# Mixer: weight casts issued apart from their low parts, with the decays, the gate's sigmoid and the first state in another order; X's scale in the FFNs on VectorE

## The chip, the cores and the metric

The kernel runs on one core of one Trainium2 chip. The metric is the time of one execution in device microseconds, the median of several runs.

## The reference

Two layers, each with the same weights for 128 context tokens and 256 latent tokens (384 in all, width 1024): an FFN, a mixer, an FFN. Every one of the three is modulated by shift, scale and gate rows made from a conditioning vector, and is closed by a LayerNorm over `alpha*x + gate*w*f(mod(x))`.

```python
def _layer(x, cond, p, lb, ctx):
    mod = (silu(cond) @ p["w_mod"] + p["b_mod"])
    sh1, sc1, g1, sh2, sc2, g2, sh3, sc3, g3 = split(mod, 9)
    f1 = _swiglu(_modulate(x, sh1, sc1), p["ffn1_w_in"], p["ffn1_w_out"])
    x = _layer_norm(ALPHA * x + 0.5 * g1 * f1, ...)
    y, new = _mixer(_modulate(x, sh2, sc2), p, lb, ctx)
    x = _layer_norm(ALPHA * x + g2 * y, ...)
    f2 = _swiglu(_modulate(x, sh3, sc3), p["ffn2_w_in"], p["ffn2_w_out"])
    return _layer_norm(ALPHA * x + 0.5 * g3 * f2, ...), new

def _mixer(h, p, lb, ctx):
    zq, zi, zff, zfb, zg, zglu, cq, ck, cv = split(h @ p["w_in"])
    # gated linear recurrence, forward and backward: S_t = f_t S_{t-1} + (1 - f_t) v_t^T, o_t = S_t^T q_t
    # f = lb + (1 - lb) * sigmoid(zff or zfb)
    # convolution module: depthwise_conv(glu_a * sigmoid(glu_b)), LayerNorm, silu
    # grouped-query attention with RMS norms and rotary positions
    y = concat([o_a, o_conv, o_c]) @ p["w_out"]
```

Outputs are the tokens, the new keys and values of the context, and the final states of the recurrence.

## The kernel before

All products run on TensorE in a two-part form: a float32 operand is split into a high part, a cast to the reduced type `F32R` by ScalarE (`split_to`, L584), and a low part, the rest, by VectorE (L585). A product is three matmuls per tile of 128: high by high, low by high, high by low. `aform` (L594) gives 24 matmuls of 384 columns for one weight part of 128 outputs (8 tiles deep); `entry_mm` (L638) gives 24 matmuls of 256 columns for one token tile.

The order of the instructions on TensorE, VectorE, ScalarE and GpSimd is the order of the program text. Only the DMA queue SP is ordered by the framework. Each engine works its queue strictly in that order; an instruction that waits holds what is behind it.

**FFN.** `ffn` runs over 22 units of 128 hidden columns. In unit `u` the program issues `prep(u + 1)` (casts and low parts of the next unit's gate, up and output weights), `fill(u)`, from unit 4 the scale of X (`finish_x`: six operations on the three token tiles, in every FFN but the first), then the gate and up products of the unit, `act` (silu on ScalarE L740, product `hf` on VectorE L742, cast L744 and low part L745) and the output product `out` of the unit before (L607). The products of a unit land in two PSUM banks that take turns (`wbank`).

`fill` makes the modulation rows of later sub-layers beside this. First it moves on every piece that is finished with its sum (`finish_job`: products with the selector `sel` on TensorE L212, a sum `rows` on VectorE L220, and in the unit after it transposes and two copies). Then it does as many steps of the next piece as the plan says; a step is two operations of 128x1024 on VectorE (L198 or L200). `SLOW` is two steps a unit over four units, `FAST` three, two, three.

**Mixer.** `load(g)` brings 256 columns of the input weight into one of four `raw` buffers, `prep(n)` splits half of them into weight part `W[n]` in one of four `wgu` buffers and, after an odd `n`, loads the next. `gemm(n)` multiplies part `n`. The parts in turn: 0 to 3 the two forget gates, 4 and 5 the queries `q`, 6 and 7 the gate half of the convolution's input (their sigmoid goes to `ua`), 8 to 11 values, keys and values of the attention for each token tile (`entry_mm` into `pkv`), 12 and 13 the other half of the convolution's input, 14 and 15 the output gate.

`Dec` holds the decays of one pair of heads. `sums(d)` is a running sum, a copy and a difference on VectorE and three exponentials on ScalarE; `keys` and `queries` are three and two VectorE operations per direction; `level(h)` copies keys and queries of blocks of `h` on ScalarE and scales them on VectorE. `dec[0]` goes through levels 8, 16, 32 and 64 before the loop over token tiles, `dec[1]` through 8 and 16 before it and 32 and 64 in it.

The loop `for i in range(2 * NT + 1)` (L1456 on) runs `scores(i)` (small products, then four masked copies on VectorE), `outputs(i - 1)`, two convolutions (`conv`, at i = 2 and 4) and other work. In it the first state is made: `state_turn(0)` transposes keys on TensorE and copies them to `kN` on ScalarE at i = 0, `states(0, kN)` multiplies them with the values `vN` at i = 1. `conv_load` writes the convolution's input `u` to memory and reads it back in another layout.

Of the kernel before, what the change touches and what calls it, by code (L numbers as in the profile page):

```python
# [9 lines left out]
F32 = mybir.dt.float32  # L10
F32R = mybir.dt.float32r
U8 = mybir.dt.uint8
AF = mybir.ActivationFunctionType
ALU = mybir.AluOpType
# [30 lines left out]
class Net:  # L45
# [195 lines left out]
    def fill(self, u, pool):  # L241

        for g in list(self.fin):
            if next(g, self) is self:
                self.fin.remove(g)
        for _ in range(self.plan.get(u, 0)):
            self.step(*self.todo.pop(0), pool)
# [248 lines left out]
    def finish_tok(self, gb, tok):  # L496
        x = self.X[:, tok, :]
        self.nc.gpsimd.tensor_tensor(x, x, gb[:, 0, :], ALU.mult)
        self.nc.gpsimd.tensor_tensor(x, x, gb[:, 1, :], ALU.add)
# [160 lines left out]
    def ffn(self, l, st, eps, nxt, fillers):  # L660
# [5 lines left out]
        with self.tc.tile_pool(name=self.name("ffn"), bufs=1, reuse_waits="tile") as fp:  # L666
# [103 lines left out]
            for u in range(2, NU):  # L770
                if u + 1 < NU:
                    prep(u + 1)
                self.fill(u, fp)
                if u == 4 and (l, st) != (0, 0):
                    self.finish_x(l - (st == 0), 2 if st == 0 else 1)
                wg, wu, _ = wsp[u]
                pg, pu = self.wbank(), self.wbank()
                self.aform(pg[:, 0:T], wg)
                if u == 2:
                    if not first:  # L780
                        turn01(1)
                        turn01(2)
                        acc = [self.pair(i) for i in self.ord]
                self.aform(pu[:, 0:T], wu)
                if u == NU - 1 and nxt is not None:
                    res = nxt(0)
                act(u, pg[:, 0:T], pu[:, 0:T])
                if first and u in (3, 6):
                    if u == 3:
                        rest = self.setup2(fp)  # L790
                    next(rest, None)
                if u == 2 and not first:
                    out(0, range(NT))
                if u - 1 < NU - hold and not (first and u == 2):
                    out(u - 1, range(NT))
            self.fill(NU, fp)
# [16 lines left out]
    def mixer(self, l, eps, nxt):  # L813
# [19 lines left out]
        def load(g):  # L833
            raws[g] = self.t(self.rawp, [P, KT, 256], "raw")
            nc.sync.dma_start(raws[g].rearrange("p k n -> p (k n)"), wi[l, cols[g]])

        def prep(n, lo, pool=None):
            g, i = divmod(n, 2)
            src = raws[g][:, 4 * i : 4 * i + 4, :] if g in (4, 5, 7) else raws[g][:, :, i * P : i * P + P]
            W[n] = self.split(pool or self.wgu, src, "wgu", lo)  # L840
            if i == 1 and g + 4 < len(cols):
                load(g + 4)

# [139 lines left out]
        for n in range(4):  # L983
            lc = slice(2 * l + n % 2, 2 * l + n % 2 + 1)
            nc.scalar.activation(
                sgf[:, n, :], sgf[:, n, :], AF.Ln, scale=self.lb1[:, lc], bias=self.lb[:, lc]
            )
        nc.vector.tensor_scalar_max(sgf, sgf, LN_MIN)
# [281 lines left out]
        prep(7, nc.vector)  # L1270
        dec[0].keys(0, E[0])
        E.append(dec[1].sums(0))
        gemm(5, ps=pq[:, 1, :])
        nc.scalar.copy(q[:, 1, :], pq[:, 1, :])
        prep(8, nc.vector)
        dec[0].keys(1, E[1])
        E.append(dec[1].sums(1))
        prep(9, nc.vector)
# [3 lines left out]
        gemm(7, ps=pu[:, 1, :])  # L1282
        for d in range(2):
            dec[0].queries(d)
        dec[0].level(8)
        nc.scalar.activation(ua[:, :, 0:T], pu, AF.Sigmoid)
        exp_table()
        prep(10, nc.vector)
        prep(11, nc.vector)
# [11 lines left out]
        two = lambda c, lo, hi: pkv[c][:, 0, :].rearrange("p (t n) -> p t n", t=2)[:, :, lo:hi]  # L1301
        nc.scalar.copy(vN[:, 0:2, :], two(0, 0, 256))
        nc.scalar.copy(vN[:, 2, :], pkv[0][:, 1, 0:256])
        prep(12, nc.vector)
        prep(13, nc.vector)
# [3 lines left out]
        nc.scalar.copy(kv[:, 2, :], pkv[1][:, 1, P:256])  # L1309
        for tok in range(NT):  # L1310
            k_ss.append(head_ssq(kn[:, tok, :], 2, self.t(mp, [P, P], "t1k", bufs=2)))
        cw = self.t(self.rawp, [P, 2048], "raw")
        nc.sync.dma_start(cw, a["conv_blk"][l])
        cw = cw.rearrange("p (a j m c) -> p a j m c", a=2, j=4, m=8)
        for ct in range(2):
            ps = gemm(12 + ct)
            nc.vector.tensor_mul(u[:, ct, 15:143], ps[:, 0:P], ua[:, ct, 0:P])
            nc.vector.tensor_mul(u[:, ct, 158:414], ps[:, P:T], ua[:, ct, P:T])
            conv_load(ct)
        dec[1].keys(0, E[2])  # L1320
        dec[1].keys(1, E[3])
        for d in range(2):
            dec[1].queries(d)
        dec[1].level(8)
        dec[1].level(16)
# [26 lines left out]
        S1s = []  # L1352

# [102 lines left out]
        for i in range(2 * NT + 1):  # L1456
            if i < 2 * NT:
                scores(i)
            if i in (1, NT + 1):
                S1s.append(states(i // NT, kN))  # L1460
            if i in (0, NT):
                kN = state_turn(i // NT)
# [143 lines left out]
    def run(self):  # L1606
        def plan(u0, *patterns):
# [5 lines left out]
            (0, 2): ([(0, 8)] + [(1, p) for p in range(4)], plan(3, FAST, FAST, SLOW, SLOW, SLOW)),  # L1613
# [110 lines left out]
```

## Time and profile before

| what | value |
|---|---|
| median of 3 runs | 1592.35 us (1592.04 to 1595.43) |
| profiled execution | 1594.68 us, span 1592.9 us |
| TensorE matmul busy | 1528.8 us, 96% of the span |
| VectorE busy | 1083.6 us, 68% |
| ScalarE busy | 615.3 us, 39% |
| GpSimd busy | 127.6 us, 8% |
| mean granted clock of TensorE | 0.982 |

The table shows each engine's busy time in the one profiled execution. Matmul ends are modelled, so a busy TensorE is not TensorE at its peak. The first layer's mixer lies between about 320 and 545 us of the span, the second's between about 1100 and 1325; the four FFNs lie around them. A granted clock of 1 is 2.4 GHz, one of 0.5 is 1.2 GHz.

### The profile page before, as it was taken

The numbers are of one execution on the slowest core, as the hardware profiler recorded it, in microseconds if no ns is written. First come the engines' busy times: TensorE is split into PE (matmuls) and PEld (weight loads), VectorE is DVE, ScalarE is ACT, GpSimd is POOL, SyncE is SP. The second block draws the span as 40 slices with busy tenths as digits, with TensorE's granted clock in tenths as the row PEclk, the third lists the DMA queues.
The fourth block names the chain that finished last, engine by engine and source line by source line (L and its number), as shares of the span: only waits on it lengthen the run. The fifth ranks groups of instructions, "written<-read, shape, count | busy, mean of one in ns | idle before, by whom it ended". The sixth has DMA issues, their size and how long they took to land.

```text
span 1592.9 us, 24588 instructions
## 1 busy us (share of the span) xinstructions
PE 1528.8 (96%) x10079; PEld 1375.4 (86%) x10079; DVE 1083.6 (68%) x1518; ACT 615.3 (39%) x1071; POOL 127.6 (8%) x123
## 2 busy tenths in 40 slices
PE   6999999998899999999999999999988999999997
PEld 5989999897677998899989999998985779999996
DVE  4788878677666798777776777765756675654335
ACT  2333222366365622333253323224643745232231
POOL 0000000120002040000013000001200023000001
PEclk9999999998899999999999999999989999999999
DMA  9776756412434456664534566542326034543411
GB/s 360 268 262 222 262 191 246 159 62 106 92 108 159 158 177 234 225 221 176 212 132 184 206 219 200 205 167 93 117 72 177 28 132 173 224 150 141 158 54 40
DMA packets 63080, 269.71 MB, mean 169 GB/s; under 512 B 9128, under 2 KB 13688, under 8 KB 47864
## 3 DMA queue, kind: packets, MB, share of 16 engines
q1 hardware_dynamic: 62968, 268.15, 47.9%
q8 instruction: 79, 1.29, 0.3%
q14 instruction: 33, 0.27, 0.1%
HBM read 265.09 MB, written 3.03 MB: 168 GB/s over the span
## 4 chain that ended last, share of the span: by engine, by line
PE 73%; DVE 14%; ACT 4%; DMA 4%; issue 4%; SPq 0%; POOL 0%; DVEq 0%; POOLq 0%; ACTq 0%
PE w L594 37%; PE d L607 19%; PE d L638 7%; DVE G L200 3%; DVE wgu L585 2%; DMA raw<-ffn_w_out 2%; PE w L946 2%; ACT wgu L584 2%; DMA raw<-w_mod_first 1%; DMA raw<-ln_b 1%; PE w L638 1%; PE w L413 1%; DVE wo L585 1%; PE w L212 1%; PE d L1170 1%
## 5 line engine op out<-in xcount | busy, mean ns | idle before, releaser
L594 PE MATMUL w<-xh,wgu 128*128 128x384 f32 x2752 | 719.6, 336 | 5.8 <-DVE hf L742 3.5
L594 PEld LDWEIGHTS w<-xh,wgu 128*128 128x128 f32 x2752 | 498.6, 188 | 16.4 <-DVE hf L742 6.4
L594 PE MATMUL w<-xl,wgu 128*128 128x384 f32 x1376 | 460.3, 335 | 0.0
L585 DVE TENSOR_TENSOR wgu<-raw,wgu 128x1024 fp32r<-128x1024 f32 (+2 forms) x218 | 258.4, 1223 | 71.6 <-ACT wgu L584 71.3
L607 PE MATMUL d<-wo,hh 128*128 128x512 f32 x1056 | 284.5, 391 | 0.1
L200 DVE SCALAR_TENSOR_TENSOR G<-t,cc,G 128x1024 f32<-128x1024 f32 x224 | 281.6, 1318 | 0.0
L594 PEld LDWEIGHTS w<-xl,wgu 128*128 128x128 f32 x1376 | 258.6, 188 | 2.2
L607 PEld LDWEIGHTS d<-wo,hh 128*128 128x128 f32 x1056 | 196.8, 188 | 36.9 <-ACT hh L744 0.4
L584 ACT CAST wgu<-raw 128x1024 fp32r<-128x1024 f32 (+2 forms) x228 | 224.7, 1031 | 7.0 <-DMA raw<-ffn_w_in 5.0
L742 DVE TENSOR_TENSOR hf<-w,sg 128x384 f32<-128x384 f32 x80 | 44.5, 557 | 223.0 <-PE w L594 223.0
L744 ACT CAST hh<-hf 128x384 fp32r<-128x384 f32 x82 | 42.1, 514 | 372.1 <-DVE hf L742 372.1
L607 PE MATMUL d<-wo,hl 128*128 128x512 f32 x528 | 163.2, 390 | 0.0
L740 ACT ACTIVATE sg<-w 128x384 f32<-128x384 f32 x80 | 39.3, 491 | 291.3 <-PE w L594 291.3
L638 PE MATMUL d<-wgu,xh 128*128 128x256 f32 x672 | 119.4, 293 | 11.5 <-ACT wgu L584 8.4
L585 DVE TENSOR_TENSOR wo<-raw,wo 128x1024 fp32r<-128x1024 f32 x90 | 109.7, 1220 | 16.9 <-ACT wo L584 16.9
L607 PEld LDWEIGHTS d<-wo,hl 128*128 128x128 f32 x528 | 99.1, 188 | 21.2
L638 PEld LDWEIGHTS d<-wgu,xh 128*128 128x128 f32 x672 | 100.8, 199 | 14.2 <-ACT wgu L584 9.6
L584 ACT CAST wo<-raw 128x1024 fp32r<-128x1024 f32 x90 | 94.2, 1048 | 20.4 <-DMA raw<-ffn_w_out 17.8
L585 POOL TENSOR_TENSOR wgu<-raw,wgu 128x1024 fp32r<-128x1024 f32 x10 | 24.8, 2498 | 772.6 <-DVE colB L400 530.6
L745 DVE TENSOR_TENSOR hl<-hf,hh 128x384 fp32r<-128x384 f32 x82 | 47.2, 576 | 47.6 <-ACT hh L744 47.6
L638 PE MATMUL d<-wgu,xl 128*128 128x256 f32 x336 | 78.0, 290 | 0.0
L422 ACT ACTIVATE t<-w,colB,colA 128x128 f32<-128x128 f32 x120 | 43.6, 468 | 41.0 <-PE w L413 35.4
(270 smaller groups left out, 1431.7 us busy)
## 6 DMA issues: line engine op xcount, KB each, us to landing
raw<-ffn_w_in SPq DMA_DIRECT2D x88, 1024.0 KB
t<-w_mod SPq DMA_DIRECT2D x128, 512.0 KB
raw<-ffn_w_out SPq DMA_DIRECT2D x44, 1024.0 KB
raw<-w_in SPq DMA_DIRECT2D x20, 1024.0 KB
raw<-w_mod_first SPq DMA_DIRECT2D x8, 1024.0 KB
G<-gates SPq DMA_DIRECT2D x12, 512.0 KB
raw<-w_out SPq DMA_DIRECT2D x8, 512.0 KB
raw<-w_out SPq DMA_DIRECT2D x4, 1024.0 KB
```

The source lines that it names most:

```text
L200: nc.vector.scalar_tensor_tensor(ac, raw, cc, ac, ALU.mult, ALU.add)
L422: self.nc.scalar.activation(m[:, k, :], pts[k // 4][:, k % 4 * P : (k % 4 + 1) * P], AF.Identity, scale=A[:, k, c : c + 1], bias=B[:, k, c ...
L584: nc.scalar.copy(w[:, 0], src)
L585: lo_engine.tensor_tensor(w[:, 1], src, w[:, 0].bitcast(F32), ALU.subtract)
L594: nc.tensor.matmul(ps, w[:, wi, k, :], x[:, k, :], start=(k == 0 and i == 0), stop=(k == KT - 1 and i == 2),)
L607: nc.tensor.matmul(acc[:, n, :], h, w[:, wi, n * 512 : n * 512 + 512], start=(first and i == 0), stop=(last and i == 2),)
L638: self.nc.tensor.matmul(ps[c], x[:, k, tsl], w[c][k // 4][:, wi, k % 4, :], start=(k == 0 and i == 0), stop=(k == KT - 1 and i == 2),)
L740: nc.scalar.activation(sg, pg, AF.Silu)
L742: nc.vector.tensor_mul(hf, pu, sg)
L744: nc.scalar.copy(hh, hf)
L745: nc.vector.tensor_sub(hl, hf, hh.bitcast(F32))
L946: nc.tensor.matmul(pc_[32 * j : 32 * j + 32, :], cw[:, ct, j, m, :], U[ct][:, j, 4 * m : 4 * m + OW], start=(m == 0), stop=(m == 7), tile_ ...
```

## The change

In the mixer `prep` is divided into `hi(n)`, the cast on ScalarE, and `lo(n)`, the low part on VectorE with the load that follows it. Casts 7 to 11 are issued ahead of their low parts, with decay work between. The two decay sums of the second pair stand after low part 9 and no longer between the keys of the first pair. Parts 12 and 13, the sigmoid and the turn of the first state come before the decays of the second pair; the convolution's products stand between the steps of these decays; the copies of the attention's keys and values come after level 8, the first state and level 16 after the second of those products.

In the FFN the first half of `fill` becomes `fill_ends` and is issued ahead of `prep(u + 1)`. `finish_x` is issued in unit 3, not 4, and its six operations are VectorE's, not GpSimd's. The plan of the first layer's second FFN begins at unit 4 with three fast pieces, not at unit 3 with two.

```diff
--- before.py
+++ after.py
@@ -238,11 +238,14 @@
             nc.vector.tensor_copy(cv[:, :, b, :], pv[:, :, b, 0:2])
         self.cols[(l, p)] = col
 
-    def fill(self, u, pool):
+    def fill_ends(self):
 
         for g in list(self.fin):
             if next(g, self) is self:
                 self.fin.remove(g)
+
+    def fill(self, u, pool):
+
         for _ in range(self.plan.get(u, 0)):
             self.step(*self.todo.pop(0), pool)
 
@@ -495,8 +498,8 @@
 
     def finish_tok(self, gb, tok):
         x = self.X[:, tok, :]
-        self.nc.gpsimd.tensor_tensor(x, x, gb[:, 0, :], ALU.mult)
-        self.nc.gpsimd.tensor_tensor(x, x, gb[:, 1, :], ALU.add)
+        self.nc.vector.tensor_tensor(x, x, gb[:, 0, :], ALU.mult)
+        self.nc.vector.tensor_tensor(x, x, gb[:, 1, :], ALU.add)
 
     def bnd_gain(self, r, st, gb):
 
@@ -768,10 +771,11 @@
             self.fill_begin(fp, 4 if nxt is not None else 3, *fillers)
             self.fill(1, fp)
             for u in range(2, NU):
+                self.fill_ends()
                 if u + 1 < NU:
                     prep(u + 1)
                 self.fill(u, fp)
-                if u == 4 and (l, st) != (0, 0):
+                if u == 3 and (l, st) != (0, 0):
                     self.finish_x(l - (st == 0), 2 if st == 0 else 1)
                 wg, wu, _ = wsp[u]
                 pg, pu = self.wbank(), self.wbank()
@@ -793,7 +797,7 @@
                     out(0, range(NT))
                 if u - 1 < NU - hold and not (first and u == 2):
                     out(u - 1, range(NT))
-            self.fill(NU, fp)
+            self.fill_ends()
             if nxt is not None:
                 res = nxt(1, res)
 
@@ -834,12 +838,23 @@
             raws[g] = self.t(self.rawp, [P, KT, 256], "raw")
             nc.sync.dma_start(raws[g].rearrange("p k n -> p (k n)"), wi[l, cols[g]])
 
-        def prep(n, lo, pool=None):
+        def hi(n, pool=None):
             g, i = divmod(n, 2)
             src = raws[g][:, 4 * i : 4 * i + 4, :] if g in (4, 5, 7) else raws[g][:, :, i * P : i * P + P]
-            W[n] = self.split(pool or self.wgu, src, "wgu", lo)
+            W[n] = self.t(pool or self.wgu, [P, 2] + list(src.shape[1:]), "wgu", F32R)
+            nc.scalar.copy(W[n][:, 0], src)
+            return src
+
+        his = {}
+
+        def lo(n, src=None):
+            nc.vector.tensor_sub(W[n][:, 1], src or his.pop(n), W[n][:, 0].bitcast(F32))
+            g, i = divmod(n, 2)
             if i == 1 and g + 4 < len(cols):
                 load(g + 4)
+
+        def prep(n, eng, pool=None):
+            lo(n, hi(n, pool))
 
         def gemm(n, half=None, ps=None):
             if ps is None:
@@ -985,6 +1000,7 @@
             nc.scalar.activation(
                 sgf[:, n, :], sgf[:, n, :], AF.Ln, scale=self.lb1[:, lc], bias=self.lb[:, lc]
             )
+        his[7] = hi(7)
         nc.vector.tensor_scalar_max(sgf, sgf, LN_MIN)
 
         S0 = self.t(hp, [P, 2, 2, 64], "S0")
@@ -1267,26 +1283,27 @@
         nc.scalar.copy(q[:, 0, :], pq[:, 0, :])
         exp_table()
         E = [dec[0].sums(0), dec[0].sums(1)]
-        prep(7, nc.vector)
-        dec[0].keys(0, E[0])
-        E.append(dec[1].sums(0))
+        his[8] = hi(8)
+        lo(7)
         gemm(5, ps=pq[:, 1, :])
         nc.scalar.copy(q[:, 1, :], pq[:, 1, :])
-        prep(8, nc.vector)
+        dec[0].keys(0, E[0])
+        lo(8)
+        his[9] = hi(9)
         dec[0].keys(1, E[1])
-        E.append(dec[1].sums(1))
-        prep(9, nc.vector)
+        lo(9)
+        E += [dec[1].sums(0), dec[1].sums(1)]
 
         pu = self.pair(2)[:, :, 0:T]
         gemm(6, ps=pu[:, 0, :])
         gemm(7, ps=pu[:, 1, :])
+        his[10] = hi(10)
+        his[11] = hi(11)
         for d in range(2):
             dec[0].queries(d)
         dec[0].level(8)
-        nc.scalar.activation(ua[:, :, 0:T], pu, AF.Sigmoid)
-        exp_table()
-        prep(10, nc.vector)
-        prep(11, nc.vector)
+        lo(10)
+        lo(11)
 
         k_ss = []
         pkv = [self.pair(0), self.pair(1)]
@@ -1299,30 +1316,38 @@
         dec[0].level(32)
         dec[0].level(64)
         two = lambda c, lo, hi: pkv[c][:, 0, :].rearrange("p (t n) -> p t n", t=2)[:, :, lo:hi]
+        prep(12, nc.vector)
+        prep(13, nc.vector)
+        nc.scalar.activation(ua[:, :, 0:T], pu, AF.Sigmoid)
+        exp_table()
         nc.scalar.copy(vN[:, 0:2, :], two(0, 0, 256))
         nc.scalar.copy(vN[:, 2, :], pkv[0][:, 1, 0:256])
-        prep(12, nc.vector)
-        prep(13, nc.vector)
+        cw = self.t(self.rawp, [P, 2048], "raw")
+        nc.sync.dma_start(cw, a["conv_blk"][l])
+        cw = cw.rearrange("p (a j m c) -> p a j m c", a=2, j=4, m=8)
+        kN = state_turn(0)
+        dec[1].keys(0, E[2])
+        dec[1].keys(1, E[3])
+        for d in range(2):
+            dec[1].queries(d)
+
+        def glu(ct):
+            ps = gemm(12 + ct)
+            nc.vector.tensor_mul(u[:, ct, 15:143], ps[:, 0:P], ua[:, ct, 0:P])
+            nc.vector.tensor_mul(u[:, ct, 158:414], ps[:, P:T], ua[:, ct, P:T])
+            conv_load(ct)
+
+        glu(0)
+        dec[1].level(8)
         nc.scalar.copy(kn[:, 0:2, :], two(1, 0, P))
         nc.scalar.copy(kn[:, 2, :], pkv[1][:, 1, 0:P])
         nc.scalar.copy(kv[:, 0:2, :], two(1, P, 256))
         nc.scalar.copy(kv[:, 2, :], pkv[1][:, 1, P:256])
+        glu(1)
+        S1s = [states(0, kN)]
+        dec[1].level(16)
         for tok in range(NT):
             k_ss.append(head_ssq(kn[:, tok, :], 2, self.t(mp, [P, P], "t1k", bufs=2)))
-        cw = self.t(self.rawp, [P, 2048], "raw")
-        nc.sync.dma_start(cw, a["conv_blk"][l])
-        cw = cw.rearrange("p (a j m c) -> p a j m c", a=2, j=4, m=8)
-        for ct in range(2):
-            ps = gemm(12 + ct)
-            nc.vector.tensor_mul(u[:, ct, 15:143], ps[:, 0:P], ua[:, ct, 0:P])
-            nc.vector.tensor_mul(u[:, ct, 158:414], ps[:, P:T], ua[:, ct, P:T])
-            conv_load(ct)
-        dec[1].keys(0, E[2])
-        dec[1].keys(1, E[3])
-        for d in range(2):
-            dec[1].queries(d)
-        dec[1].level(8)
-        dec[1].level(16)
         nc.sync.dma_start(self.o["new_cache_v"][0, l].rearrange("s h d -> s (h d)"), kv[:, 0, :])
 
         wop, wraw = {}, {}
@@ -1349,8 +1374,6 @@
 
 
         dm = self.pair(0)
-        S1s = []
-
         def keys_turn():
             pt = self.wbank()
             for i, src in enumerate((kn[:, 0, :], ck[:, 0, :], kn[:, 1, :], kn[:, 2, :])):
@@ -1456,10 +1479,10 @@
         for i in range(2 * NT + 1):
             if i < 2 * NT:
                 scores(i)
-            if i in (1, NT + 1):
-                S1s.append(states(i // NT, kN))
-            if i in (0, NT):
-                kN = state_turn(i // NT)
+            if i == NT + 1:
+                S1s.append(states(1, kN))
+            if i == NT:
+                kN = state_turn(1)
             if i == 2 * NT:
                 keys_turn()
             if i == 0:
@@ -1610,7 +1633,7 @@
 
         fill = {
             (0, 0): ([(0, p) for p in range(2, 8)], plan(1, SLOW, FAST, FAST, FAST, FAST, SLOW)),
-            (0, 2): ([(0, 8)] + [(1, p) for p in range(4)], plan(3, FAST, FAST, SLOW, SLOW, SLOW)),
+            (0, 2): ([(0, 8)] + [(1, p) for p in range(4)], plan(4, FAST, FAST, FAST, SLOW, SLOW)),
             (1, 0): ([(1, p) for p in range(4, 8)], plan(4, *[SLOW] * 4)),
             (1, 2): ([(1, 8)], plan(4, [1] * 8)),
         }
```

## Rows read from the trace of the kernel before

**Rows 1.** Waits of TensorE from 355 to 470: engine, tile, line, releaser; us, times, longest
```profile
PE w L1091 <- ACT kN L1083: 4.0, 1, 4.0
PE d L638 <- ACT wgu L584: 3.9, 2, 2.4
...
PE d L594 <- ACT q L1267: 0.9, 1, 0.9
```

**Rows 2.** Stretches: length, then busy time of each engine, then the clock
```profile
379.00:382.00 3.00, 2.59 (x11) 2.29 (x11) 2.70 (x6) 0.17 (x1) 0.00 (x0) 0.50 0.00 0
1094.00:1098.00 4.00, 2.37 (x15) 1.75 (x15) 1.86 (x3) 1.77 (x4) 0.74 (x2) 1.00 0.75 305
```

**Rows 3.** ScalarE in order of time: start, us, line, tiles, count, idle before
```profile
361.75 0.46 ACT L1267 COPY q<-d 128x384 f32<-128x384 f32 x1
...
369.72 1.03 ACT L584 CAST wgu<-raw 128x1024 fp32r<-128x1024 f32 x1
```

**Rows 4.** VectorE in order of time, first layer's mixer
```profile
368.01 0.56 DVE L1030 TENSOR_TENSOR sk<-sk,em 128x384 f32<-128x384 f32 x1
...
371.93 0.61 DVE L1042 SCALAR_TENSOR_TENSOR sk<-E,lb,sk 128x384 f32<-128x384 f32 x1
...
373.21 0.95 DVE L1025 TENSOR_TENSOR_SCAN sk<-rmask,sk 128x384 f32<-128x384 f32 x1
...
384.01 1.23 DVE L585 TENSOR_TENSOR wgu<-raw,wgu 128x1024 fp32r<-128x1024 f32 x1 [2.21 <-ACT wgu L584]
385.15 0.55 DVE L1048 TENSOR_TENSOR sk<-sk,q 128x384 f32<-128x384 f32 x1
...
387.28 0.35 DVE L1063 TENSOR_TENSOR da<-da,et 128x192 f32<-128x192 f32 x1
...
394.63 0.35 DVE L1063 TENSOR_TENSOR da<-da,e 128x192 f32<-128x192 f32 x1
...
398.24 0.16 DVE L1066 TENSOR_TENSOR e<-e 128x3 f32<-128x3 f32 x1
...
418.99 1.58 DVE L1145 COPY_PREDICATED A<-smask,d 128x256 f32<-128x256 uint8 x4
```

**Rows 5.** The chain that ended last: start, us, engine, tile, line, count
```profile
330.40 8.64 PE d L638 x72
...
420.62 0.69 PE d L1170 x4
...
422.75 7.41 PE w L946 x64
...
436.18 5.50 PE w L946 x64
...
654.48 8.33 PE w L594 x48
662.81 4.11 PE d L607 x18
```

**Rows 6.** GpSimd and VectorE in order of time, second FFN of the first layer
```profile
557.33 3.21 POOL L498 TENSOR_TENSOR X<-X,raw 128x1024 f32<-128x1024 f32 x1 [25.36 <-DMA raw<-ln_g]
...
563.82 13.44 DVE L200 SCALAR_TENSOR_TENSOR G<-t,cc,G 128x1024 f32<-128x1024 f32 x4
577.19 0.55 DVE L742 TENSOR_TENSOR hf<-w,sg 128x384 f32<-128x384 f32 x1
...
582.68 4.87 DVE L200 SCALAR_TENSOR_TENSOR G<-t,cc,G 128x1024 f32<-128x1024 f32 x4
```

**Rows 7.** Waits of TensorE from 540 to 820; the first row: the whole run
```profile
PE w L594 <- DVE rows L220: 2.3, 3, 0.8
...
PE w L594 <- DVE rows L220: 1.6, 2, 0.8
...
PE w L594 <- DVE hf L742: 1.3, 1, 1.3
...
PE w L212 <- DVE G L200: 0.8, 2, 0.5
```


## The prediction

> **What bounds the kernel now.** I read three views: TensorE's waits by stretch, the clock by stretch, and then the order of VectorE and ScalarE around the waits. TensorE works almost without a break, so only a wait of TensorE or a half-speed stretch can give time back; both lie in the mixer, between the product `gemm(4)` and the second convolution, once per layer. In the first layer TensorE waits there for weight casts (3.9 us), for the turned state `kN` (4.0) and for the copy of `q` (0.9) [rows 1]. After the first of these waits the granted clock is 0.50, the lower of its two levels, while a gap of 1.6 us elsewhere leaves it at 1.00 [rows 2]. VectorE and ScalarE are not full there, but they take turns: before the cast of part 7 ScalarE stands behind the exponentials of the decay sums, and its low part stands behind the cast [rows 3, 4]. So what ends TensorE's waits is the order in two in-order queues. The second layer repeats this (same waits; 59.7 us against 59.3 for the same span of work), so I cost one layer and double it.
>
> **Part 1, casts apart from low parts, `gemm(5)` to `gemm(13)`.** I walk the new order forward from the end of `gemm(4)` at 361.3 us, with durations of the trace.
> ScalarE: the cast of part 7 (1.03) now stands directly after the logarithms, before the copy of `q` that began at 361.75 [rows 3]. The copy therefore ends about 1.0 later, at 363.2, and `gemm(5)`, which waits for that copy today, starts at 363.3: its wait grows from 0.94 to 1.95. That is the price of this part. What is queued behind the cast on ScalarE, the table load and a dummy, has until 366.9 and is covered.
> VectorE: after the second decay sum, at 368.6 [rows 4], the low part of 7 can run at once, because its cast is long done: it ends at 369.7 instead of 372.0. Behind it stand keys 1.3 (371.93 to 373.21), low part 8 at 1.15 (384.01 to 385.15), keys 1.3, low part 9 at 1.15: that ends at 374.5. Casts 8 and 9 end at 370.8 and 372.1 on ScalarE, in time. Then two decay sums of a scan 0.95, a copy and a difference 0.56 (374.5 to 378.0), queries 2.1 (385.15 to 387.28) to 380.1, a wait of 1.2 for ScalarE, which has casts 10 and 11 ahead of the copies of level 8, level 8 itself to 382.9, low parts 10 and 11 to 385.15.
> TensorE: three products of 4.17 (half of 8.33 [rows 5]) run from 363.3 to 375.8; parts 8 and 9 are ready by 374.5, so the first token-major group follows at once and takes 8.64 [rows 5], to 384.5; part 10 is ready at 384.0 and part 11, needed a sixth of the group later at 385.9, at 385.15. No wait, with margins of 0.5 and 0.75 us, the smallest of the walk. The second group ends at 393.1. Today it ends at 402.8: 9.7 us.
>
> **Part 2, the first state changed and the gate's sigmoid later.** VectorE does levels 16 to 64 (3.8 us, 394.63 to 398.4 [rows 4]) to 388.95, low parts 12 and 13 to 391.3. ScalarE loads a table, does the sigmoid and loads the other table until 393.6, copies the values, and copies the turned keys at 395.0. The table loads are as many as before; they lie beside the two groups of products, as before. TensorE: transposes 0.65, products 12 and 13 8.35, to 402.15. The sigmoid and both weights are early by 3 us or more. VectorE does the keys and queries of the second pair (4.7) to 396.0, under product 12; in-order, it then holds level 8 until product 12 has ended, and the state's update and level 16 until product 13 has.
> Then the states (0.6; the wait of 4.0 is gone) and the scores of two tokens (1.45 each) to 405.75. The output of the first token needs the masks of VectorE: after product 13 there stand 0.7, the state's update 0.4, level 16 with the copies of ScalarE 1.6, the sums of squares 0.95, and the masks 1.5 (1.58 for the four [rows 4]), to 407.45. TensorE waits 1.75 there. So the first output starts at 407.5 against 420.6 [rows 5]: **13.1 us**. Check by work alone: 12.5 + 17.3 + 0.65 + 8.35 + 0.6 + 2.9 = 42.3 of products, and waits 1.95 and 1.75, give 46.0 from 361.3.
> SP's queue: the loads of the next weights and of the convolution's blocks wait for low parts that now come earlier; the write of the new values and the writes of the state are moved past each other, and both are ready before the reads of `u` for the second convolution, which has 13 us more to come; the load of the convolution's input starts about 2 us after `u` is written, at 401, and has taken about 6 us, so it lands near 407, and the convolution begins at 409.3. A cover of 2 us; if it is gone, its excess is added to each layer.
> The first convolution took 7.41 at partly half clock and the second 5.50 [rows 5]; without the long wait I take 5.50, and 0.5 for the small products around it: 2.4. **One layer gains 15.5.** In the second, 15.8 by the same walk, less a gap of 1.3 that no wait explains and that may stay: 14.9 as a middle.
>
> **Part 3, X's scale by VectorE.** Where GpSimd scales X beside VectorE, VectorE's four steps took 13.44 us against 4.87 for four undisturbed, and GpSimd's own took 3.21 [rows 6]. VectorE then came late and TensorE waited 1.3, and in the units behind it 0.8 and 1.6 [rows 7]. After: six operations of 1.22 (a product of two such tiles, like a low part), 7.3 us of VectorE in unit 3. The three steps that stood there begin a unit later. The loads of scale and offset land at 558.2 at the latest, when VectorE gets there, so its wait is 0; it ends at 565.5, before its product needs it at 568.0. In the other two FFNs the place is also filled without delay and TensorE waits for nothing there today: 0. Gain 3.7.
>
> **Part 4, `fill_ends` before the weights.** The sum of a finished piece on VectorE now stands ahead of the three low parts of the unit, and it waits for products that TensorE starts only after the output product (4.11 [rows 5]) of the unit before. VectorE stands about 3.4 us in each of 16 such units, with low parts, steps and the unit's gate product queued behind. From a gate product to the first step VectorE takes 5.5 (577.19 to 582.68), two steps 4.8 [rows 6]: 10.3 of TensorE's 12.46 in a unit of two steps, 12.7 in one of three. A group of three units, with eight steps of which the first is 1.1 cheaper, makes 35.1 of TensorE's 38.7, with the wait 39; but late time shortens the wait, so lateness stays near 1.8 us. TensorE asks for that gate product only 8.3 us after its own (4.11 + 4.17). So 0 lost. Gained: the wait for these rows, 2.3 over the run [rows 7], of which 1.6 is in part 3; 0.7 more.
>
> **Sum.** 15.5 + 14.9 + 3.7 + 0.7 = 34.8. The profiled execution took 1594.68 (span 1592.9 and 1.8 around it), 2.3 above the median of the runs: 1559.9 by it, 1557.6 by the median. I say **1559**.
>
> **Rivals.** *The clock falls at the new gaps.* The gaps of 1.95 and 1.75 lie between one of 1.6 that left the clock at 1.00 and the waits that brought it to 0.50 [rows 2]; I take the nearer, no fall. If it falls at both, the price is 1.9 after the first (a convolution's difference [rows 5]) and 2.4 after the second: 4.3 a layer, 1568. The Trainium skill, page "TensorE: Matmul & The Clock Gate", section "Why this matters for your kernels", says that idle gaps between bursts of matmuls bring the clock back down. [...] Of the waits that are there today the trace agrees [rows 2]; for gaps of this size no run here shows it. Against it: a like stretch of small products at 430 to 436 is followed by a convolution of 5.50 [rows 5]. Chance 0.2.
> *VectorE becomes late*: the margins of 0.5 to 0.75 fail, or the masks come later than 407.5. Bound from above by the wait that is there now, 4.0 a layer [rows 1]: 1567. Against it: the walk uses in-order sums of measured durations. 0.1.
> *The change does not do what it says*: the casts find no free buffer, or a wait on a whole tile holds them where they were. Then only the 4.0 per layer for `kN` and part 3 and 4 remain, 12.4: 1582. Against it: the buffers' last readers end at least 3 us before each cast but that of part 11 (375.8, cast at 380). 0.05.
> *Slower*: part 4's wait on VectorE is paid by TensorE. It decides when a gate product comes over 7.7 us late; from there each of 16 units costs up to 3.4, 54 in all: 1594.7 - 34.8 + 54 = 1614. Against it: lateness does not add up while three units need 35 of 38.7. 0.03.
>
> **How the numbers follow.** Forecast 0.60, rivals 0.2, 0.1, 0.05, 0.03, and 0.02 for better: both remaining gaps hidden, 7.4 more, 1552. The range takes the forecast, the first two rivals, together at most 1576, and the better end: 1553 to 1574. A measurement of this kernel tells about 0.2% from no change: faster 0.94, same 0.03, slower 0.03.
>
> **What would show it.** Right: no wait of TensorE for `wgu` in the token-major products and none for `kN`; a wait of about 2 for `q`, one of about 1.8 for the masks; clock 1.00 through both; convolutions of 5.50; no GpSimd operation on X and no stretched step. Wrong: a wait of TensorE for parts 10 or 11, for `raw` in the convolution, or for a gate product in the FFN; or a clock under 1.00 there.

## The result, and the profile after

The changed kernel took 1558.16 us (median of 4 runs, 1556.16 to 1559.67) against 1593.89 for the kernel before on the same chip (1592.04 to 1596.25): a ratio of 0.9774, 95% interval 0.9755 to 0.9794. Its profiled execution took 1557.95, span 1556.2. The two spans differ by 36.7 us, and the trace says in which stages. The marks are the end of `gemm(4)` and the start of the second convolution in each layer:

| stretch | before | after | gain | forecast |
|---|---|---|---|---|
| start to the end of `gemm(4)`, first layer | 361.3 | 359.8 | 1.5 | 0.7 |
| from there to the second convolution | 74.8 | 59.5 | 15.3 | 15.5 |
| to the end of `gemm(4)`, second layer (two FFNs) | 706.0 | 700.9 | 5.1 | 3.7 |
| from there to the second convolution | 75.0 | 61.0 | 14.0 | 14.9 |
| to the end | 375.8 | 375.0 | 0.8 | 0 |
| sum | 1592.9 | 1556.2 | 36.7 | 34.8 |

The mixers end earlier than the section on the profile before has it: TensorE's first transposes of the next FFN stand at 518 and 1299 us in the kernel before, not at 545 and 1325, and at 501 and 1263 in the changed one.

TensorE's waits in the first mixer, 340 to 470 us (waiting operation, releaser: us in total, times, longest), answer to [rows 1]:

```profile
PE d L597 <- ACT q L1283: 1.9, 1, 1.9
PE d L1186 <- DVE A L1161: 1.2, 2, 0.8
PE d L1152 <- issue: 0.6, 1, 0.6
```

The waits for casts (3.9) and for `kN` (4.0) are gone, and with them 2.2 us of waits for low parts, which [rows 1] leaves out; in the kernel before they were

```profile
PE d L638 <- DVE wgu L585: 1.6, 2, 0.9
...
PE d L594 <- DVE wgu L585: 0.6, 1, 0.6
```

In their place stand the wait for `q`, twice as long as before, and one for the masks (`issue` is idle time for which the profile shows no releaser). ScalarE's order shows why the first grew; it answers to [rows 3]:

```profile
360.28 1.03 ACT L845 CAST wgu<-raw 128x1024 fp32r<-128x1024 f32 x1
361.22 0.47 ACT L1283 COPY q<-d 128x384 f32<-128x384 f32 x1
```

The cast of part 7 stands ahead of the copy, one cast long. VectorE's low parts 10 and 11, the sums of squares and the masks stand as follows (to be read against [rows 4]):

```profile
380.98 2.35 DVE L851 TENSOR_TENSOR wgu<-raw,wgu 128x1024 fp32r<-128x1024 f32 x2
...
403.18 0.47 DVE L889 TENSOR_REDUCE ss<-t1k 128x2 f32<-128x128 f32 x2
403.83 0.29 DVE L889 TENSOR_REDUCE ss<-t1k 128x2 f32<-128x128 f32 x1 [0.18 <-ACT t1k L888]
404.03 1.58 DVE L1161 COPY_PREDICATED A<-smask,d 128x256 f32<-128x256 uint8 x4
```

The masks come one by one, and TensorE goes on as they come. The output products that waited, and the two convolutions, against [rows 5]:

```profile
404.85 0.44 PE L1186 MATMUL d<-A,vN 128*64 128x128 f32 x4 [0.84 <-DVE A L1161]
405.67 0.44 PE L1186 MATMUL d<-A,vN 128*64 128x128 f32 x4 [0.38 <-DVE A L1161]
407.13 5.74 PE L961 MATMUL w<-raw,raw 128*32 128x399 f32 x64
419.29 5.57 PE L961 MATMUL w<-raw,raw 128*32 128x399 f32 x64
```

By this view the convolutions take 5.74 and 5.57, where they took 7.48 and 5.57 before.

The waits are only about half of what the first layer gained. The stretch from `gemm(4)` to the second convolution, before and after (columns as in [rows 2]: length, then TensorE's busy time; the granted clock is the third number from the end):

```profile
361.30:436.10 74.80, 63.61 (x777) 53.47 (x776) 50.56 (x127) 33.82 (x77) 2.67 (x6) 0.86 0.37 105
```

```profile
359.80:419.30 59.50, 55.77 (x779) 50.76 (x778) 50.10 (x127) 33.38 (x77) 4.45 (x6) 1.00 0.46 131
```

TensorE's idle time fell by 7.5 us (from 11.2 to 3.7) and its busy time by 7.8, for the same products: the mean granted clock rose from 0.86 to 1.00. In the second layer busy time fell by 4.9 of the 14.0.

The clock was not everywhere at its upper level, though. Four stretches, the first two of the first layer, the others of the second: the gap ahead of `gemm(5)`, the products behind it, and the products behind the same gap in the second layer:

```profile
359.80:361.80 2.00, 0.07 (x2) 0.07 (x1) 1.97 (x3) 1.98 (x4) 0.00 (x0) 1.00 0.85 279
362.00:364.00 2.00, 2.00 (x13) 2.00 (x13) 1.97 (x3) 1.20 (x2) 0.00 (x0) 1.00 1.02 401
1122.00:1124.00 2.00, 1.87 (x6) 1.87 (x7) 1.97 (x3) 1.58 (x3) 0.00 (x0) 0.55 0.99 401
1124.00:1126.00 2.00, 2.00 (x9) 2.00 (x8) 1.93 (x4) 0.36 (x1) 0.00 (x0) 0.59 1.04 434
```

The same gap of 1.93 us was followed by 1.00 in one layer and by the lower level, 1.2 GHz, in the other. Added up over the last two stretches, 2 x 0.45 + 2 x 0.41, that cost 1.7 us.

In the FFNs between the mixers (470 to 1110 us), against [rows 7], the waits for `rows` and `G` and the one of 1.3 for `hf` are gone; the 5.5 for X lie at the FFNs' starts and ends, and the kernel before has them too:

```profile
PE w L416 <- DVE X L482: 5.5, 3, 2.5
PE w L597 <- DVE hf L745: 0.5, 1, 0.5
```

### The profile page after: what moved, and what is told of

Read it like the earlier page. It is cut to its first block, busy times and chain, and to the rows that moved or that the text cites. A ratio compares the mean times of both kernels' runs of the same rounds, so it can differ in the third digit from the quotient of the medians.

```text
span 1556.2 us, 24567 instructions
## 1 busy us (share of the span) xinstructions
PE 1512.5 (97%) x10079; PEld 1369.2 (88%) x10079; DVE 1085.7 (70%) x1536; ACT 614.1 (39%) x1071; POOL 81.4 (5%) x105
## 4 chain that ended last, share of the span: by engine, by line
PE 85%; DVE 6%; ACT 3%; DMA 3%; issue 2%; POOL 0%; SPq 0%; DVEq 0%; POOLq 0%; ACTq 0%
PE w L597 44%; PE d L610 22%; PE d L641 8%; DMA raw<-w_mod_first 2%; PE d L597 2%; PE w L961 1%; PE w L641 1%; PE w L416 1%; PE w L212 1%; PE d L1152 1%; DVE G L200 1%; PE d L1186 1%; PE d L1405 1%; DMA raw<-ffn_w_out 1%; PE d L1453 1%
## 5 line engine op out<-in xcount | busy, mean ns | idle before, releaser
L200 DVE SCALAR_TENSOR_TENSOR G<-t,cc,G 128x1024 f32<-128x1024 f32 x224 | 272.9, 1279 | 0.0
L588 DVE TENSOR_TENSOR wgu<-raw,wgu 128x1024 fp32r<-128x1024 f32 (+2 forms) x186 | 215.1, 1198 | 39.9 <-ACT wgu L587 39.5
L587 ACT CAST wgu<-raw 128x1024 fp32r<-128x1024 f32 (+2 forms) x196 | 191.9, 1029 | 6.9 <-DMA raw<-ffn_w_in 4.8
L743 ACT ACTIVATE sg<-w 128x384 f32<-128x384 f32 x80 | 39.2, 491 | 309.8 <-PE w L597 309.8
L641 PE MATMUL d<-wgu,xh 128*128 128x256 f32 x672 | 112.5, 284 | 0.0
L641 PEld LDWEIGHTS d<-wgu,xh 128*128 128x128 f32 x672 | 96.3, 191 | 0.4
L597 PE MATMUL d<-xh,wgu 128*128 128x384 f32 x192 | 54.1, 356 | 6.1 <-ACT q L1283 3.9
```

The lines of the kernel that those rows point to most:

```text
L200: nc.vector.scalar_tensor_tensor(ac, raw, cc, ac, ALU.mult, ALU.add)
L587: nc.scalar.copy(w[:, 0], src)
L588: lo_engine.tensor_tensor(w[:, 1], src, w[:, 0].bitcast(F32), ALU.subtract)
L597: nc.tensor.matmul(ps, w[:, wi, k, :], x[:, k, :], start=(k == 0 and i == 0), stop=(k == KT - 1 and i == 2),)
L641: self.nc.tensor.matmul(ps[c], x[:, k, tsl], w[c][k // 4][:, wi, k % 4, :], start=(k == 0 and i == 0), stop=(k == KT - 1 and i == 2),)
L743: nc.scalar.activation(sg, pg, AF.Silu)
```

## The experiments

My theory was the prediction's sum: the mixers carry 30.4 us, the FFN 4.4. The rivals were that one half of the mixer's change does all of it, that the clock falls at the gaps that are left, and that VectorE's new wait in the FFN costs TensorE. All ratios are to the kernel before on the same chip.

| kernel | median us (lowest to highest) | ratio, 95% interval |
|---|---|---|
| e1 mixer only | 1564.0 (1561.9 to 1565.1) | 0.9818, 0.9794 to 0.9843 |
| e2 FFN only | 1587.7 (1585.5 to 1589.9) | 0.9971, 0.9957 to 0.9984 |
| e3 casts only | 1575.3 (1574.8 to 1576.4) | 0.9888, 0.9868 to 0.9908 |
| e4 state only | 1582.6 (1580.5 to 1585.3) | 0.9934, 0.9909 to 0.9958 |
| e5 X on GpSimd | 1556.1 (1555.6 to 1557.4) | 0.9767, 0.9754 to 0.9781 |
| e6 ends after | 1559.9 (1558.7 to 1560.7) | 0.9789, 0.9776 to 0.9802 |
| e7 two casts | 1559.7 (1557.2 to 1562.8) | 0.9795, 0.9782 to 0.9809 |
| e8 cast 7 later | 1557.6 (1556.6 to 1561.6) | 0.9780, 0.9767 to 0.9794 |
| e9 own bank | 1556.0 (1553.7 to 1558.0) | 0.9768, 0.9752 to 0.9784 |
| e10 bank, squares | 1556.5 (1554.1 to 1559.5) | 0.9778, 0.9762 to 0.9794 |
| e11 steps back | 1559.2 (1557.9 to 1559.8) | 0.9785, 0.9772 to 0.9799 |
| e12 low part 10 first | 1553.3 (1550.5 to 1556.0) | 0.9751, 0.9735 to 0.9766 |

**Halves.** e1 is the changed kernel with the FFN of before; e2 the kernel before with the changed FFN.

> The change to the mixer alone; the FFN is that of before (X's scale on GpSimd, pieces finished late). My theory: the two mixers carry 15.5 + 14.9 of the 34.8 us, so about 1563 us, and the waits for X (1.3) and the units behind it in the second FFN return. Rival, the FFN's part is worth more than its own waits because a late FFN moves the start of the next mixer: 1566 or more.

> The mixer of before, with the change to the FFN alone (X's scale on VectorE in unit 3, finished pieces ahead of the weights). My theory: 3.7 + 0.7 = 4.4 us, so about 1589.5 us; the mixer keeps its waits for casts (3.9) and for kN (4.0). If the two halves add up, its gain and that of the mixer alone make that of the whole change, 35.7 us by the medians. Rival, VectorE standing for finished pieces costs TensorE: no gain or a loss, and waits for a gate product.

The medians are 1564.0 for 1563 expected and 1587.7 for 1589.5. Savings of 1.82% and 0.29% make 2.11% against 2.26% for the whole: within the intervals they add up, and the mixers carry most of it, as forecast.

**The mixer's two parts.** e3 takes the changed first half and the old second half; e4 the reverse.

```diff
 # e3: the second half as before, so the sigmoid stays early
         ...
         dec[0].level(8)
+        nc.scalar.activation(ua[:, :, 0:T], pu, AF.Sigmoid)
+        exp_table()
         lo(10)
         ...
```

> The casts issued apart from the low parts and the new order of the decays, alone; the first state, the loop over tokens, the place of the gate's sigmoid and the FFN are those of before. My theory: the second token-major group ends 9.7 us earlier per layer, of which the wait for kN (4.0) stays, so 9 to 10 a layer, about 1574 us. The convolution behind the wait for kN still takes about 7.4, because that wait still brings the clock to its lower level. Rival, the gain comes from the earlier state, and casts alone only move the wait to kN: 2 to 4 us a layer, about 1587.

> The first state changed early (turn of the keys, state, masks ahead of the loop over tokens), alone; casts and low parts in the order of before, the sigmoid in its old place, FFN of before. My theory: the wait for kN (4.0) goes, a wait of 1 to 2 for the masks stays, and the waits for the casts (3.9) and the slow clock behind them stay: 3 to 6 us a layer, 1582 to 1588 us. Rival, the earlier casts are needed for it, because VectorE reaches the keys and the masks late: no gain, 1593.

The medians are 1575.3 for about 1574 expected and 1582.6 for 1582 to 1588. Savings of 1.12% and 0.66% make 1.78% against e1's 1.82%. By the trace, from `gemm(4)` to the second convolution a layer of e3 is 9.7 and 8.5 us shorter than before, one of e4 5.9 and 4.0. In e3 the wait for `kN` stays; the first convolution behind it runs slowly, as before:

```profile
PE w L1103 <- ACT kN L1095: 4.0, 1, 4.0
...
411.54 7.41 PE L957 MATMUL w<-raw,raw 128*32 128x399 f32 x64
```

In e4 the waits for the casts stay, and the clock behind them is 0.50 (380 to 382 us). So both rivals fall: each half removes its own wait and the slow clock behind it. In e4's second layer the clock fell again, behind the masks' gaps (1.7 us), which is most of the 1.9 between its two layers.

**X and the steps (part 3).** e5 puts X back on GpSimd, in the new unit; e11 leaves X on VectorE and puts the steps back.

```diff
 # e5
-        self.nc.vector.tensor_tensor(x, x, gb[:, 0, :], ALU.mult)
+        self.nc.gpsimd.tensor_tensor(x, x, gb[:, 0, :], ALU.mult)
         ... (the offset likewise)
 # e11
-plan(4, FAST, FAST, FAST, SLOW, SLOW)
+plan(3, FAST, FAST, SLOW, SLOW, SLOW)
```

> The whole change, but X's scale and offset back on GpSimd, in the new unit 3. My theory: VectorE's steps beside them stretch again (13.4 us for four instead of 4.9) and VectorE is late for one unit; TensorE pays 1 to 4 us over the run, 1559 to 1562 us. Rival, the unit itself was what mattered (one earlier): no loss, 1558.

> The whole change, X on VectorE in unit 3, but the steps of the next columns are left where they were: they begin in unit 3 again instead of unit 4, so three steps (6.1 us) stand with X (7.3 us) in one unit. Theory, after the run with X on GpSimd cost nothing: the free unit is what pays, not the engine; here VectorE is some 3 us late for the next gate product, and TensorE's waits for hf, rows and G return in part, 1 to 4 us: 1559 to 1562. Rival, it is the engine (no port shared with GpSimd): no loss, 1558.

I expected 1 to 4 us of loss in each. e5's median, 1556.1, shows none. e11's, 1559.2, lies at the lower end of what I expected, but its interval overlaps the changed kernel's, and the trace shows no loss in this FFN; so both theories fall. The length of the second FFN, from its first transposes to the next stage's (the 1.7 us of a fallen clock at its start taken off where it fell), is 290.8 to 292.1 in the four kernels with the FFN of before (before, e1, e3, e4) and 285.7 to 286.3 in the ten others, e5 and e11 among them. In e5 VectorE, with no steps in that unit, stands idle for 10.1 us while GpSimd works; only one low part is caught:

```profile
548.47 2.41 POOL L501 TENSOR_TENSOR X<-X,raw 128x1024 f32<-128x1024 f32 x1
550.96 2.60 POOL L502 TENSOR_TENSOR X<-X,raw 128x1024 f32<-128x1024 f32 x1
...
549.08 0.56 DVE L745 TENSOR_TENSOR hf<-w,sg 128x384 f32<-128x384 f32 x1 [10.13 <-PE w L597]
...
551.22 3.43 DVE L588 TENSOR_TENSOR wgu<-raw,wgu 128x1024 fp32r<-128x1024 f32 x1
```

That low part took 3.43: the 2.34 for which GpSimd's operation still ran (until 553.56), and 1.1 of its own. In e11 VectorE works from 541.1 to 554.4 without a break and comes to the gate product 3 us later than in the changed kernel, and TensorE waits for nothing:

```profile
542.44 4.87 DVE L200 SCALAR_TENSOR_TENSOR G<-t,cc,G 128x1024 f32<-128x1024 f32 x4
547.22 1.22 DVE L501 TENSOR_TENSOR X<-X,raw 128x1024 f32<-128x1024 f32 x1
...
553.27 1.23 DVE L502 TENSOR_TENSOR X<-X,raw 128x1024 f32<-128x1024 f32 x1
554.41 0.55 DVE L745 TENSOR_TENSOR hf<-w,sg 128x384 f32<-128x384 f32 x1
```

What cost 5 us was the coincidence of GpSimd's X with VectorE's steps [rows 6]. Moving either away is enough; the change does both. That X moved one unit earlier could be a third cure, since e5 and e11 both keep unit 3, and no run has GpSimd's X there beside the steps. The rows speak against it: GpSimd waits for its load, and in e5 it starts 37.6 us after the FFN's first transposes, against 37.5 before (39.2 less the 1.7 of the fallen clock); so its X would still run beside steps that begin in unit 3 (38.4 in e11).

**Finished pieces (part 4).** e6 sums them behind the unit's weights again.

> The whole change, but finished pieces are summed behind the unit's weights, as before. My theory: the standing of VectorE for the sums (13 times, 38 us) goes and TensorE's waits for rows (2.3 us over the run) return: 1558.5 to 1560.5 us. Rival, VectorE's standing costs TensorE something hidden in the FFN units: 1555 or less.

The wait of 0.7 for `rows` returns in the first FFN (40 to 345 us):

```profile
PE w L594 <- DVE rows L220: 0.7, 1, 0.7
```

It stands in all five kernels that sum behind the weights (before, e1, e3, e4, e6) and in none of the other nine. It does not return in the second, whose length is the same (286.2); there those waits came from VectorE's lateness. VectorE's standing, 38 us over the run, costs TensorE nothing that the traces show. By the medians part 4 can't be told from nothing.

**The gap at `q` and the clock.** e7 casts part 8 too ahead of the copy of `q`; e8 casts part 7 behind it.

```diff
 # e7
         his[7] = hi(7)
+        his[8] = hi(8)
 # e8
-        his[7] = hi(7)
         ...
         exp_table()
+        his[7] = hi(7)
```

> The whole change, with the casts of parts 7 and 8 both ahead of the copy of q, which widens TensorE's wait for q from 1.95 to about 3 us. It tells how wide a gap the clock bears at this place. My theory of a clock that falls after the longer waits: the granted clock of the products behind it drops below 1.00 and the layer loses 1.0 for the gap and 1 to 3 for the clock, 1562 to 1566 us. Rival, the clock fell in the kernel before for another reason than the wait's length: it stays at 1.00 and only the gap is paid, 1560.

> The whole change, with the cast of part 7 behind the copy of q and the table load. My theory: the wait for q goes back to 0.9, and the cast still ends before 368.6 us, when VectorE comes to its low part: 1.0 us a layer better, 1556 us. Rival, the cast falls behind the exponentials of the decay sums again and the low parts shift by more than the margins of 0.5 and 0.75 us at parts 10 and 11: same or worse, 1558 to 1562.

The waits came out as expected, 2.9 and 0.9 (0.75 in the second layer of e8), and the stretch to the second convolution in the first layer is 60.4, 58.5, and 59.5 in the changed kernel. The times are not apart: intervals overlap, and 2 us are covered by what the clock does. e7's median, 1559.7, is its rival's 1560 and not the 1562 to 1566 of its theory; e8's, 1557.6, lies between theory and rival, and a wait of 0.3 and 0.5 for a low part, which its rival named, did appear. Over all traces with a mixer like this one, a gap of 1.9 at `q` was followed by the lower clock in 7 of 12 layers (after, e1, e3, e5, e6, e11), one of 2.9 in 1 of 2, gaps of 0.75 to 1.0 in none of 8. The masks' two gaps (0.84 and 0.38) were followed by it in 5 of 18 layers, the one of 0.38 alone in none of 4. Each of these falls cost 1.7 us. The gaps at the starts of the FFNs, where TensorE waits for X, say the same: 41 gaps of 1.3 to 1.6 were followed by no fall, one of 2.0 by one, and of 28 gaps of 2.5 15 were. So the prediction's theory, that the clock holds at these gaps, and e7's, that it falls, are both too simple: the length shifts the odds, and what else decides stays open.

**Closing the gaps.** e9 gives `gemm(5)` a bank of its own, e10 also moves the sums of squares behind low part 15, e12 also puts low part 10 ahead of level 8.

```diff
 # e9
-        gemm(5, ps=pq[:, 1, :])
-        nc.scalar.copy(q[:, 1, :], pq[:, 1, :])
+        p5 = gemm(5)
+        nc.scalar.copy(q[:, 1, :], p5)
 # e12, besides
+        lo(10)
         dec[0].level(8)
-        lo(10)
         lo(11)
```

> The whole change, with gemm(5) writing a bank of its own in place of the second half of the bank that q's copy is reading. My theory: TensorE doesn't wait for q's copy at all, the 1.9 us gap closes, but parts 10 and 11 were ready only 0.5 and 0.75 us ahead of their products, so 0.5 to 1.9 a layer comes out: 1554 to 1557 us, and a wait for part 10 of up to 1.3 appears. Rival, the gap is needed by another thing (a weight, a free bank) and only changes its name: 1558.

> As the kernel with gemm(5) in a bank of its own, and the keys' sums of squares behind the low part of 15 instead of ahead of the masks. My theory: the wait for the masks shrinks from 1.2 to about 0.3 us a layer: 1.8 us less than with the bank alone. Rival, the masks wait for the decays or their copies on ScalarE, or the sums are then needed too early: no further gain.

> As the kernel with gemm(5) in its own bank and the sums of squares later, and the low part of 10 ahead of level 8, in the 1.3 us in which VectorE waits for ScalarE's copies. Theory: TensorE's wait for part 10 (1.4 a layer) goes to 0 and no gap over 0.5 us is left between gemm(4) and the second convolution but that without a named wait; 2.5 us less than the kernel before it, about 1554 by the median, and no stretch under clock 1.00 in the mixers. Rival, part 11 is then late, or the part's wait moves to the scores or the masks: no gain, 1556.

In e9 the wait for `q` is gone, and part 10 is late instead, by nearly what I expected:

```profile
PE d L641 <- DVE wgu L851: 1.3, 1, 1.3
PE d L1186 <- DVE A L1161: 1.2, 2, 0.8
```

In e10 the wait for the masks is 0.4, as expected, but the 1.8 us did not show in its time (1556.5 against e9's 1556.0, and the intervals overlap). In e12 the wait for part 10 is gone. From `gemm(4)` to the second convolution e12 takes 57.7 in both layers (59.5 and 61.0 in the changed kernel). All its runs lie below all runs of the changed kernel, but the two were measured apart, and the intervals of the ratios overlap (0.9735 to 0.9766 against 0.9755 to 0.9794), so a gain of some 3.6 us (0.23%) is likely, not settled. One expectation failed: in the second layer a gap that no releaser explains was followed by a convolution at the lower clock:

```profile
1173.75 0.21 PE L1152 MATMUL d<-db 64*64 64x64 f32 x1 [1.60 <-issue]
1174.51 7.25 PE L961 MATMUL w<-raw,raw 128*32 128x399 f32 x64
```

A gap of this kind, 0.2 to 1.7 us among the small products of the state and the scores, stands in one layer at least of every version, before too; its cause stays open.

## Why the prediction was right, step by step

**Part 1 held.** `gemm(5)` waited 1.93 (1.95 forecast). The second token-major group had no wait, and e9 shows that its margin was real and about as thin as walked: with `gemm(5)` 1.9 earlier, part 10 is 1.3 late, so it had 0.6 to spare (0.5 forecast). e3 prices the part: 9.7 us in the first layer, as walked, and 8.5 in the second, where the clock fell at `q`.

**Part 2 held.** The second half of the first output, the one at 420.62 before [rows 5], starts 45.9 after `gemm(4)` (46.2 forecast). The wait for the masks was 1.2, not 1.75: I let TensorE wait for all four masks, and it goes on as they come, one by one. The covers that I named (the weights, the sigmoid, the load of the convolution's input) all held: no wait of TensorE names them. The second convolution starts 59.5 after `gemm(4)`, 15.3 earlier than before, for 15.5 forecast.

**The step that failed is the clock.** I took 1.00 through both gaps by the nearer row, a gap of 1.6 elsewhere [rows 2]. In the second layer of the profiled execution the clock fell, which I had named as a sign of being wrong, and cost 1.7. The layer came out 0.9 short and not 1.7, because other differences between the two traces go the other way; among them, the waits for casts that went were longer there (4.5 us against 3.9), and the unexplained gap shrank from 1.3 to 0.8. The forecast for that layer was off by a little too: the middle of 14.5 and 15.8 is 15.2, not 14.9.

The rows did not support my reading either. I put the new gaps between one of 1.6 that left the clock up and "the waits that brought it to 0.50". The low clock before begins at 378.8, and ahead of it stand two gaps, each shorter than 1.95:

```profile
377.61 0.39 PE L638 MATMUL d<-wgu,xh 128*128 128x256 f32 x1 [1.45 <-ACT wgu L584]
378.87 0.58 PE L638 MATMUL d<-wgu,xh 128*128 128x256 f32 x1 [0.87 <-DVE wgu L585]
```

The same trace has the lower clock behind both gaps of 2.5 at the starts of FFNs, so half-speed stretches did not lie in the mixer alone, and a chance of 0.2 for a fall was too low. My price for a fall, 1.9 after the first gap, was near (1.7); what was wrong was to treat it as all or nothing. With 7 of 12 and 5 of 18, an execution loses 2 x 0.58 x 1.7 + 2 x 0.28 x 1.7 = 2.9 us on average, an estimate from a few traces. The Trainium skill, page "TensorE: Matmul & The Clock Gate", section "Why this matters for your kernels", says that idle gaps between bursts of matmuls bring the clock back down, but speaks of gaps longer than any in the changed mixer. Here the measurement differs: the clock fell in 7 of 12 layers behind the gap of 1.9.

**Part 3 was right in place and too small.** I counted the listed waits, 3.7 us; the second FFN became 5 us shorter. Between its first transposes and the next stage's, length and TensorE's busy time were, in the kernel before and in the changed one (the first two numbers behind the stretch):

```profile
520.50:811.00 290.50, 285.41 (x1609) 263.12 (x1609) 223.03 (x240) 95.42 (x141) 25.80 (x14) 1.00 0.56 200
```

```profile
503.70:789.00 285.30, 283.97 (x1609) 263.10 (x1609) 217.16 (x245) 96.01 (x142) 7.01 (x8) 1.00 0.58 203
```

Idle time fell from 5.1 to 1.3 us, which is about the 3.7; the other 1.4 is time that the profile counts as work of TensorE for the same 1609 products. Some 0.5 of it is the lower clock at the FFN's start, of which the first stretch holds 1.7 us and the second 0.7. The rest lies at the same waits: by the starts of the same products in both traces, TensorE lost 1.6, 2.2 and 1.1 at the three places where the waits are 1.3, 1.6 and 0.8. At the first:

```profile
576.16 0.34 PE L594 MATMUL w<-xh,wgu 128*128 128x384 f32 x1
577.79 0.45 PE L594 MATMUL w<-xh,wgu 128*128 128x384 f32 x1 [1.29 <-DVE hf L742]
```

Undisturbed, such products start 0.17 us apart and are shown as 0.33 long, so each overlaps the next. The idle time counts from the end of the earlier one; from start to start, 1.63, this stop took 1.46 more than usual. A sum of listed waits is thus a lower bound of their price. My account of the mechanism, GpSimd stretching VectorE's steps, is shown by [rows 6], e5 and e11. That the move of X to VectorE was needed for it is not: the new place of the steps alone does as much. The Trainium skill, page "SBUF — State Buffer", section "SBUF: two separate sides", says that the two engines share a pair of ports under an exclusive lock: whichever starts first has it for its whole instruction, and the other waits. The low part of 3.43 in e5 agrees.

**Part 4** gave the 0.7 that I named, and the standing of VectorE (3.4 us at the longest, as forecast) cost nothing, so the rival on the slower side falls. It stood 13 times and not 16. The other two rivals fall with the rows above: no cast was held, TensorE waited for no low part, and the masks came no later than walked.

The gains beyond the forecast, 0.8 ahead of the first mixer and 0.8 behind the last, are not the change's for sure. The end of `gemm(4)` in the first layer is at 356.9 in e5 and 359.8 in the changed kernel, whose code up to there is the same. The last stretch of the kernel before holds a fall of the clock (1300 to 1304 us, 1.7 us) that the changed kernel has not. So the time came out within 1 us of the forecast partly by luck: the stages missed by +0.8, -0.2, +1.4, -0.9 and +0.8 us, and the clock's average loss of 2.9 was not in the sum.

## What to carry to other kernels

When an engine off the critical path makes the bound one wait, walk its in-order queue with measured durations: issuing casts apart from the subtractions that need them, with the decay sums later, gave 17 to 18 us here (e3) with no work saved. Where one step is moved away from a collision, look whether another edit already does it; two cures for one collision pay once. And after such a change the small gaps that remain are worth more than their length, because some of them cost the clock as well: in the first layer about half of the gain came with the clock.

## What I had not expected of the hardware

The clock's answer to a gap is not fixed by the gap's length: 1.93 us of idle left it at 1.00 in one layer and at its lower level in the other layer of the same execution, and two gaps of 0.84 and 0.38 with four short products between them were followed by a fall in 5 of 18 layers. A GpSimd product of two 128x1024 tiles took 2.4 us beside an idle VectorE (e5) and 2.7 to 3.4 beside a working one (3.21 in [rows 6]); VectorE's low part in e5 took 2.34 until the GpSimd operation had ended and 1.1 behind it, about its usual length.
